# Retention's output made feature-major, and its chain cut into steps between the next head's projections

## The chip, the cores and the metric

One core of a Trainium2 chip. The metric is the device time of the whole program in microseconds, here the median of three runs. A core has five engines with a queue each, worked off in order: TensorE (PE, with its weight loads as PEld), VectorE (DVE), ScalarE (ACT), GpSimd (POOL) and SyncE (SP), which only issues DMA. Granted clock is the share of TensorE's 2.4 GHz that it was given; 0.5 is 1.2 GHz.

## The reference

Two layers of a hybrid model on 512 latent and 256 context tokens of width 1024. Each layer mixes tokens by three branches (retention, window attention, a Fourier transform), joins them by gates, and then sends each token through two of 32 experts. The change touches retention alone: eight heads of width 64, in two directions.

```python
inner = einsum('bcihd,bcjhd->bchij', qc, kc) * dec          # chunks of 128 tokens
o_inner = einsum('bchij,bcjhe->bcihe', inner, vc)
u = einsum('bcjhd,jh,bcjhe->bchde', kc, zeta, vc)           # state of a chunk
_, s_prev = lax.scan(step, s0, moveaxis(u, 1, 0))           # s -> g_chunk * s + u
o_cross = einsum('bcihd,ih,bchde->bcihe', qc, xi, s_prev)
...
mu = mean(o, axis=-1); var = mean(square(o - mu), axis=-1)  # per head
on = (o - mu) * rsqrt(var + 1e-5)
ret = silu(g) * on
```

Layer 0 computes this for all 768 tokens (six chunks), layer 1 for the 512 latent ones (four chunks); the keys and values of the context are used in both.

## The kernel before

All work stands in one program without a loop over layers. Tiles come from pools with a fixed number of buffers: `big` has 20 units of 8 KB per partition, PSUM has 8 banks (3 for projections, `mm`; 2 for `sc`; 2 for transposes, `tr`; 1 for `ov`). The order in which each engine's instructions stand is set by a list scheduler that goes by program order as priority and by when it thinks an operand is ready, so neighbouring pieces of the program are mixed.

A projection (`proj`, L275 to L277) multiplies 128 columns of `w_in`, split into two float32r parts, with the normed tokens: 24 products of 512 latent columns and, where the context is wanted, 24 of 256. In layer 0 each projection also takes one step of the adaLN sums (L149, four products of 32 columns by 512, added up by DVE in L199).

Heads go in pairs `p` = 0 to 3. `ret_proj(p)` makes four projections: keys and queries (rotated by DVE and POOL, L286 to L289), values (turned to token-major by six transposes, L296), and the gate. `ret_chain(p)` then computes the output: it turns the keys (L296), weighs the values for the states (L444), forms q times xi on POOL (L438), the chunks' states (L452, scanned on DVE in L456 to L464), the inner scores (L473, masked with the decay in L475) and the output (L482: scores times values; L487: q times xi times the states, both adding into one PSUM tile per head, tokens on the partitions, so the moving operand has the head's 64 columns). Then the norm: means on DVE (L498, L499), centring (L502), squares on ACT (L503), their sums on DVE (L506, L507), the power -1/2 on POOL (L142), the scaling on POOL (L509), six transposes back (L514), the gate on DVE (L517), and the split into two parts for the branch product (L242, L243).

In the program `ret_proj(p + 1)` stands as a whole ahead of `ret_chain(p)`; ahead of the last chain stand attention's key and value projections and its first query projection:

```python
pr = ret_proj(0)
for p in range(4):
    nxt = ret_proj(p + 1) if p < 3 else None
    ...
    ret_chain(p, pr)
    pr = nxt
```

Of the kernel before, what the change touches and what calls it, by code (L numbers as in the profile page):

```python
# [15 lines left out]
OP = mybir.AluOpType  # L16
# [18 lines left out]
T1_MASK, T1_KA, T1_VA = 0, 384, 1152  # L35
T2_LAT, T2_CTX, T2_CF, T2_ALT, T2_ALTC, T2_ROW, T2_ROWC, T2_N = 0, 1024, 1280, 1536, 1540, 1542, 1799, 1928
CP, _o = {}, 0
for _k, _n in (("ident", 128), ("tri", 128), ("iota1", 64), ("iota0", 32), ("i64", 16), ("kcon", 96), ("tok2", 6),
               ("hbm2", 2), ("zc", 2)):
    CP[_k] = (_o, _o + _n)  # L40
    _o += _n
# [19 lines left out]
def tile_backbone(ctx: ExitStack, tc: tile.TileContext, a: dict, out: bass.AP, stop=None, dbg=None):  # L61
# [51 lines left out]
    # DRAM scratch  # L113
# [6 lines left out]
    cin = const(16, "cin", a["c"])  # L120
    cp = const(480, "cp")
# [7 lines left out]
    tok2, hbm2, zc = (cp[:, CP[k][0]:CP[k][1]] for k in ("tok2", "hbm2", "zc"))  # L129
# [39 lines left out]
    def ada_feature(l, row):  # L169
        """sh1 and norm*(1+sc1), one value for each partition: [128, stream, kc]"""  # L170
# [21 lines left out]
    def ada_steps():  # L192
# [10 lines left out]
        # the last: over a partition's rows on DVE, over the partitions on PE (one stream, the latent one)  # L203
# [42 lines left out]
    def make_h(l, xt_l, xt_c):  # L246
        """xt_*: token-major tiles, already times rstd"""
# [70 lines left out]
    decay = {}  # L318

    def decay_logs(l):  # L320
# [13 lines left out]
        Z = cst.tile([128, 16], F32, name=f"Z{l}", tag="Z")      # [h of f | h of b]  # L334
# [26 lines left out]
    # =====================================================================  # L361
    def layer(l, xt_l, xt_c):
# [15 lines left out]
        mask = t1[:, T1_MASK:T1_MASK + 384]  # L378
# [10 lines left out]
        def o_tiles(b):  # L389
            """[high, low][group] of a branch's output, feature-major"""  # L390
# [10 lines left out]
        def ret_proj(p):  # L401
# [3 lines left out]
            sgr = rv[:, 768:1536]  # L405
            pc, pl = proj(l, p * 4, both)
# [10 lines left out]
            to_tokens(vtok, lambda i: (vc[:, i * 128:i * 128 + 128] if i < 2 else vl[:, (i - 2) * 128:(i - 1) * 128]),  # L417
                      ((0, 2), (2, 4)))
# [4 lines left out]
            return k, q, vtok, sgr  # L423

        def ret_chain(p, st):
            k, q, vtok, sgr = st
# [3 lines left out]
            vz = rb[:, 0:1536].rearrange("p (t h d e) -> p t h d e", t=6, h=2, d=2)  # L430
            St = rc[:, 0:768].rearrange("p (t d e) -> p t d e", t=6, d=2)
            ktok = rc[:, 768:1536].rearrange("p (t c) -> p t c", t=6)
            to_tokens(ktok, lambda i: k[:, i * 128:i * 128 + 128], ((0, 2), (2, 4)))
            # q times xi, for the states' part
            qs = slice(0, 768) if full else lsl
            nt = 6 if full else 4
            for d in range(2):
# [9 lines left out]
            u = []  # L447
            for lo, n in ((0, 2), (2, 4)):
                up = pso()
                for i in range(n):  # L450
                    for h in range(2):
                        PE.matmul(up[h * 64:h * 64 + 64, i * 128:i * 128 + 128], ktok[:, lo + i, h * 64:h * 64 + 64],  # L452
                                  vz[:, lo + i, h, :, :], start=True, stop=True, skip_group_check=True)
# [12 lines left out]
            # inner products  # L466
            for lo, n in (((0, 2), (2, 4)) if full else ((2, 4),)):
                sc = [pss(), pss()]
                for i in range(n):
                    ts = slice((lo + i) * 128, (lo + i) * 128 + 128)  # L470
                    for h in range(2):
                        hs = slice(h * 64, h * 64 + 64)
                        PE.matmul(sc[h][:, i * 128:i * 128 + 128], k[hs, ts], q[hs, ts], start=True, stop=True)  # L473
                for h in range(2):
                    DVE.tensor_tensor(SD[:, h, lo:lo + n, :], sc[h][:, 0:n * 128].rearrange("p (t i) -> p t i", t=n),  # L475
                                      bmid(Dt[:, p * 2 + h, :], n), op=OP.mult)
            oo = [pss(), pss()]
            for t in TL:
                ts = slice(t * 128, t * 128 + 128)
# [909 lines left out]
```

## Time and profile before

| | |
|---|---|
| median of 3 runs | 2665.6 us (2663.58 to 2668.18) |
| profiled execution: span from first to last instruction | 2652.4 us |
| profiled execution's own time | the page gives the span alone; the median lies 13.2 us above it |
| PE busy | 2404.5 us (91%) |
| PEld busy | 1580.7 us (60%) |
| DVE, ACT, POOL busy | 1045.9, 571.0, 469.6 us |
| HBM traffic | 229 GB/s over the span |

The page's slices are 66.3 us each. The retention stage of layer 0 runs from about 56 to 360 us, that of layer 1 from about 1540 to 1730 us; the experts' weights stream from 893 us in layer 0 and again from layer 1's end of mixing to the end. A timeline row gives start, duration and number of records; a float32 product shows as two records, a transpose as one. Starts of following rows tell the pace better than durations, since records overlap. A windows row gives, for one stretch, each engine's busy time and number of records, the granted clock, the share of the DMA engines and the rate.

### The profile page before, as it was taken

To read this page: it belongs to the slowest core of one execution; us is meant where nothing else is said; L and a number is where in the kernel's file an instruction comes from. 1 tells how busy PE (TensorE), PEld (TensorE's weight loads), DVE (VectorE), ACT (ScalarE), POOL (GpSimd) and SP (SyncE) were. 2 spreads that over 40 slices of the span, in tenths; PEclk is the share of its full clock that TensorE was granted. 3 is DMA by queue.
4 is the path that set the end of the run, shared out by engine and by line. 5 is a ranking of instruction groups with operands and counts; after the bars stand their busy time and mean duration, and the time that the engine had idled before them with its cause. 6 is when DMAs were issued, how large, how long until landed. Compare 5 with 4: busy or idle time off the path is not lost. (4 is left out here: it accounts for less than half of the span.)

```text
span 2652.4 us, 44021 instructions
## 1 busy us (share of the span) xinstructions
PE 2404.5 (91%) x17245; PEld 1580.7 (60%) x17245; DVE 1045.9 (39%) x3181; ACT 571.0 (22%) x1285; POOL 469.6 (18%) x414
## 2 busy tenths in 40 slices
PE   5999999999999979999999599999999898997774
PEld 3777766688889944434443388766888743343221
DVE  5434445635234643233332644565335521221112
ACT  3211134521223211011110422245224200000000
POOL 0212110000222412111211123210022321121111
PEclk8988889999999979999999799999999899998897
DMA  7423211235225389899999621110235599999996
GB/s 273 162 96 108 102 51 63 81 111 209 71 64 179 138 331 417 352 371 389 415 417 411 237 72 46 58 48 21 88 97 173 207 379 417 411 410 407 416 415 253
DMA packets 129730, 594.43 MB, mean 224 GB/s; under 512 B 20940, under 2 KB 22052, under 8 KB 73968
## 3 DMA queue, kind: packets, MB, share of 16 engines
q1 hardware_dynamic: 115184, 561.92, 55.0%
q0 software_dynamic: 13376, 26.27, 2.6%
q8 instruction: 138, 2.26, 0.3%
q10 hardware_dynamic: 960, 3.39, 0.3%
q14 instruction: 72, 0.59, 0.1%
HBM read 579.74 MB, written 28.25 MB: 229 GB/s over the span
## 5 line engine op out<-in xcount | busy, mean ns | idle before, releaser
L1079 PE MATMUL mm<-w_gu,xT 128*32 128x256 f32 (+1 forms) x3776 | 564.4, 505 | 85.1 <-DMA w_gu<-in_w_gu_dram 81.7
L1079 PEld LDWEIGHTS mm<-w_gu,xT 128*32 128x32 f32 (+1 forms) x3776 | 192.0, 127 | 390.8 <-issue 227.4
L275 PE MATMUL mm<-hH,hl 128*128 128x512 f32 x800 | 319.7, 401 | 1.7 <-DVE shuf L287 0.9
L276 PE MATMUL mm<-hL,hl 128*128 128x512 f32 x800 | 316.1, 395 | 0.0
L277 PE MATMUL mm<-hH,hl 128*128 128x512 f32 x800 | 315.5, 395 | 0.4 <-DVE hl L238 0.4
L238 DVE TENSOR_TENSOR hl<-raw,hl 128x512 fp32r<-128x512 f32 x248 | 183.3, 741 | 252.1 <-ACT hl L237 251.8
L1104 PE MATMUL mm<-w_d,aT 128*32 128x256 f32 (+1 forms) x1888 | 267.0, 488 | 6.9 <-DVE aT L1094 5.9
L237 ACT CAST hl<-raw 128x512 fp32r<-128x512 f32 x248 | 153.4, 620 | 385.9 <-PE mm L277 250.6
L1084 ACT ACTIVATE act<-mm 128x256 f32<-128x256 f32 (+1 forms) x87 | 30.1, 346 | 899.0 <-PE mm L1079 865.0
L1113 POOL DMA_INDIRECT y_d<-y,gd x87 | 87.7, 1008 | 742.3 <-DVE y L1112 562.3
L1104 PEld LDWEIGHTS mm<-w_d,aT 128*32 128x32 f32 (+1 forms) x1888 | 90.6, 124 | 157.0 <-issue 124.0
L1085 DVE TENSOR_TENSOR act<-act,mm 128x256 f32<-128x256 f32 (+1 forms) x87 | 32.2, 370 | 380.3 <-ACT act L1084 380.3
L275 PEld LDWEIGHTS mm<-hH,hl 128*128 128x128 f32 x800 | 151.3, 189 | 41.1 <-issue 6.1
L277 PEld LDWEIGHTS mm<-hH,hl 128*128 128x128 f32 x800 | 151.3, 189 | 35.5 <-issue 3.9
L276 PEld LDWEIGHTS mm<-hL,hl 128*128 128x128 f32 x800 | 151.2, 189 | 32.4 <-issue 5.2
L275 PE MATMUL mm<-hcH,hl 128*128 128x256 f32 x480 | 143.8, 300 | 5.8 <-ACT ra L408 3.9
L276 PE MATMUL mm<-hcL,hl 128*128 128x256 f32 x480 | 141.8, 295 | 0.0
L277 PE MATMUL mm<-hcH,hl 128*128 128x256 f32 x480 | 141.5, 295 | 0.0
L986 POOL DMA_INDIRECT xg<-h_d,gd x87 | 91.1, 1047 | 148.1 <-issue 71.2
L275 PEld LDWEIGHTS mm<-hcH,hl 128*128 128x128 f32 x480 | 96.2, 200 | 19.0 <-issue 5.7
L276 PEld LDWEIGHTS mm<-hcL,hl 128*128 128x128 f32 x480 | 96.4, 201 | 4.9 <-issue 1.2
L277 PEld LDWEIGHTS mm<-hcH,hl 128*128 128x128 f32 x480 | 96.5, 201 | 3.6 <-issue 3.1
(385 smaller groups left out, 3694.4 us busy)
## 6 DMA issues: line engine op xcount, KB each, us to landing
w_gu<-in_w_gu_dram SPq DMA_DIRECT2D x256, 1024.0 KB
w_d<-in_w_d_dram SPq DMA_DIRECT2D x128, 1024.0 KB
raw<-in_w_in_dram SPq DMA_DIRECT2D x200, 256.0 KB
wada<-in_w_ada_dram SPq DMA_DIRECT2D x48, 1024.0 KB
raw<-in_w_br_dram SPq DMA_DIRECT2D x48, 256.0 KB
yb<-y_d SPq DMA_DIRECT2D x10, 1024.0 KB
raw<-in_w_out_dram SPq DMA_DIRECT2D x32, 256.0 KB
h_d<-hb POOLq DMA_DIRECT2D x10, 512.0 KB, 6.4
```

Source lines behind the costliest of these rows:

```text
L237: ACT.copy(hl[:, 0], r)
L238: DVE.tensor_tensor(hl[:, 1], r, hl[:, 0].bitcast(F32), op=OP.subtract)
L275: PE.matmul(o[:, 0:n], wh, h[kc], start=kc == 0, stop=False)
L276: PE.matmul(o[:, 0:n], wh, lo[kc], start=False, stop=False)
L277: PE.matmul(o[:, 0:n], wl, h[kc], start=False, stop=kc == 7)
L986: POOL.indirect_dma_start(out=xg, out_offset=None, in_=h2_d[l].rearrange("r (a c) -> (r a) c", c=sz * 8), in_offset=bass.IndirectOffsetOnA ...
L1079: PE.matmul(p1[q * sz:q * sz + sz, 0:n], xT[:, k * sz:k * sz + sz], w[:, q * n:q * n + n], start=k == 0, stop=k == 7, skip_group_check=True)
L1084: ACT.activation(sv, pv[:, :, 0, :], AF.Silu)
L1085: DVE.tensor_tensor(sv, sv, pv[:, :, 1, :], op=OP.mult)
L1104: PE.matmul(p2[q * sz:q * sz + sz, 0:n], aT[:, j * 128 + q_ * sz:j * 128 + q_ * sz + sz], w[:, q * n:q * n + n], start=k == 0, stop=k == 3 ...
L1113: s = POOL.indirect_dma_start(out=y_d[l].rearrange("r (a c) -> (r a) c", c=n), out_offset=bass.IndirectOffsetOnAxis(ap=di, axis=0), in_=y, ...
```

## The change

Three things.

1. The values are turned to token-major by a product with a constant matrix, the identity less 1/64 over each head's block (`cenm`, a new table of 128 columns), where transposes stood. So the values have no mean over a head's 64 features, and neither has the output, and the steps that took the mean (L498, L499, L502) are gone.
2. The output comes feature-major. Scores times values has the values (128 by 64) as stationary operand and the masked scores (128 columns) as moving one; the states' part has the state (64 by 64) stationary and q times xi (128 columns) moving. Both heads of a pair add into one PSUM tile, on partitions 0 to 63 and 64 to 127. The squares (ACT, from PSUM) are averaged over each head's features by a product with a matrix of two columns (`bo`), which gives the variance token-major; DVE adds 1e-5, POOL takes the power, ACT spreads it over 64 columns, six transposes bring it to feature-major, and DVE multiplies it into the gated output that POOL has formed meanwhile.
3. `ret_proj` and `ret_chain` are generators. One step of the chain stands behind each of the next pair's four projections (behind the three of attention for the last pair), and the chain's last step behind the first projection of the pair after that. The scores of the context's chunks come a step later than those of the latent ones. The weighted values `vz` lie in the unused ends of three units, so that the masked scores no longer share their place.

"Steps" below are the parts between two `yield`s: turning the keys, `vz`, q times xi and the latent scores; states and context scores; output, squares and gating; variance and power; transposes and split.

```diff
-    def to_tokens(dst, src, segs):
+    def to_tokens(dst, src, segs, by=None):
...
-                PE.transpose(t[:, i * 128:i * 128 + 128], src(lo + i), ident)
+                if by is None:
+                    PE.transpose(t[:, i * 128:i * 128 + 128], src(lo + i), ident)
+                else:
+                    PE.matmul(t[:, i * 128:i * 128 + 128], src(lo + i), by, start=True, stop=True)
...
+        SP.dma_start(t1[:, T1_CEN:], a["t1"][:, 2432:2560])
...
+            to_tokens(vtok, lambda i: (vc[:, i * 128:i * 128 + 128] if i < 2 else vl[:, (i - 2) * 128:(i - 1) * 128]),
+                      ((0, 2), (2, 4)), cenm)
+            yield
...
+            for t in range(6):
+                vt = vtok[:, t].rearrange("p (h e) -> p h e", h=2).unsqueeze(2).broadcast_to([128, 2, 2, 64])
+                DVE.tensor_tensor(vz[t], vt, blast(zb, 64), op=OP.mult)
...
-            for h in range(2):
-                for d in range(2):
-                    j = d * 8 + p * 2 + h
-                    DVE.tensor_scalar(vz[:, :, h, d, :], vtok[:, :, h * 64:h * 64 + 64], Z[:, j:j + 1], None, op0=OP.mult)
+            inner(*segs[0])
+            yield
...
+            if full:
+                inner(*segs[1])
+            yield
+            oo = {lo: pss() for lo, n in segs}
+            for lo, n in segs:
...
-                    PE.matmul(oo[h][:, t * 64:t * 64 + 64], SD[:, h, t, :], vtok[:, t, h * 64:h * 64 + 64],
-                              start=True, stop=False, skip_group_check=True)
+                        PE.matmul(oo[lo][hs, i * 128:i * 128 + 128], vtok[:, lo + i, hs], SD[:, h, lo + i, :],
+                                  start=i == 0, stop=False, skip_group_check=True)
...
-                        PE.matmul(oo[h][:, t * 64:t * 64 + 64], qx[hs, d, ts], St[hs, t, d, :],
+                            PE.matmul(oo[lo][hs, i * 128:i * 128 + 128], St[hs, t, d, :],
+                                      qx[hs, d, t * 128:t * 128 + 128],
...
+                ACT.activation(sq[:, cs_], oo[lo][:, 0:n * 128], AF.Square)
+                ACT.copy(cen[:, cs_], oo[lo][:, 0:n * 128])
+            POOL.tensor_tensor(cen[:, qs], cen[:, qs], sgr[:, qs], op=OP.mult)
+            yield
+            vp = pso()
+            for t in TL:
+                PE.matmul(vp[:, t * 2:t * 2 + 2], sq[:, t * 128:t * 128 + 128], bo, start=True, stop=True)
...
+            DVE.tensor_scalar(var[:, t0 * 2:12], vp[:, t0 * 2:12], 1e-5, None, op0=OP.add)
+            rsqrt(var[:, t0 * 2:12], var[:, t0 * 2:12], 12 - t0 * 2)
+            ACT.copy(sq[:, qs].rearrange("p (n e) -> p n e", e=64), blast(var[:, t0 * 2:12], 64))
+            yield
...
-                DVE.tensor_reduce(mu3[:, :, h], ov, axis=AX.X, op=OP.add, negate=True)
-            DVE.tensor_scalar(mu, mu, 1.0 / 64, None, op0=OP.mult)
...
-            ACT.activation(sq, cen, AF.Square)
...
-            DVE.tensor_reduce(v3, sq, axis=AX.X, op=OP.add)
-            DVE.tensor_scalar(var, var, 1.0 / 64, 1e-5, op0=OP.mult, op1=OP.add)
-            rsqrt(var, var, 2 * n)
-            POOL.tensor_tensor(cen, cen, blast(v3, 64), op=OP.mult)
...
-                    PE.transpose(t[:, i * 128:i * 128 + 128], cf[:, lo + i, :], ident)
+                    PE.transpose(t[:, i * 128:i * 128 + 128], sq[:, (lo + i) * 128:(lo + i) * 128 + 128], ident)
...
-                DVE.tensor_tensor(f, t[:, 0:n * 128], sgr[:, seg], op=OP.mult)
+                DVE.tensor_tensor(f, t[:, 0:n * 128], cen[:, lo * 128:(lo + n) * 128], op=OP.mult)
...
+            chain = ret_chain(p, st)
+            for _ in (ret_proj(p + 1, nxt) if p < 3 else kv()):
+                if done is not None:
+                    next(done, None)
+                    done = None
+                next(chain, None)
+            st, done = nxt, chain
```

TensorE before, at the end of layer 0's first chain: the inner scores (L473) go straight over into the output products.

```order
L276 MATMUL mm_1281<-hL_282,hl_1277 128x512
L473 MATMUL sc_1119<-ra_449 128x128 x4
L482 MATMUL sc_1130<-rv_450,rb_1068 128x64
L487 MATMUL sc_1130<-rc_1069,rq_1067 128x64
L482 MATMUL sc_1130<-rv_450,rb_1068 128x64
L487 MATMUL sc_1130<-rc_1069,rq_1067 128x64
L482 MATMUL sc_1130<-rv_450,rb_1068 128x64
L487 MATMUL sc_1130<-rc_1069,rq_1067 128x64 x2
```

TensorE now, at the same place: the output products stand between the value projection of the next pair (`mm_983`), an adaLN group, and its gate projection (`mm_1095`).

```order
L277 MATMUL mm_983<-hcH_283,hl_980 128x256
L149 MATMUL ov_1033<-wada_1034,cs 32x512 x4
L500 MATMUL sc_1045<-rb_835,rv_451 64x128 x8
L500 MATMUL sc_1046<-rb_835,rv_451 64x128 x4
L509 MATMUL sc_1045<-rq_834,rc_836 64x128 x16
L509 MATMUL sc_1046<-rq_834,rc_836 64x128 x4
L275 MATMUL mm_1095<-hH_279,hl_1086 128x512
```

The two kinds of product alternated, tile by tile; now all of one kind come first, then all of the other, and a projection follows at once.

TensorE now, at the end of that chain: the variance products stand inside the key projection of the pair after the next (`mm_1195`), the transposes of the scale behind it.

```order
L275 MATMUL mm_1195<-hcH_283,hl_1187 128x256
L522 MATMUL ov_1172<-cp,rb_835 128x2 x6
L276 MATMUL mm_1195<-hcL_284,hl_1187 128x256
...
L277 MATMUL mm_1195<-hcH_283,hl_1192 128x256
L149 MATMUL ov_1247<-wada_1248,cs 32x512 x4
L455 MATMUL sc_1298<-ra_758 128x128
L455 MATMUL sc_1299<-ra_758 128x128
L455 MATMUL sc_1298<-ra_758 128x128
L532 MATMUL tr_1261<-cp,rb_835 128x128 x4
L532 MATMUL tr_1270<-cp,rb_835 128x128 x2
L455 MATMUL sc_1299<-ra_758 128x128
```

Of the 29 projection products between L522 and L532, those left out are of the same projection: 12 of 512 columns and 17 of 256 in all. Before, POOL's scaling stood between the output products and the transposes, with seven projection products and four of L473 beside it.

POOL now, from the queries' rotation of one pair to that of the next (`shuf` is the rotation's second part, `var` the power):

```order
L289 TENSOR_TENSOR ra_758<-ra_758,shuf_935 128x512
L518 TENSOR_TENSOR rb_835<-rb_835,rv_451 128x768
L142 TENSOR_TENSOR var_1179<-var_1179,mhalf 128x12
L288 TENSOR_TENSOR shuf_1255<-shuf_1255,rope_413 128x512
L289 TENSOR_TENSOR ra_1183<-ra_1183,shuf_1255 128x512
L466 TENSOR_TENSOR rq_1277<-ra_758,misc_418 128x768 x2
L288 TENSOR_TENSOR shuf_1378<-shuf_1378,rope_413 128x512
```

The scaling by the power, which stood behind L142, is gone from POOL; the gating (L518) stands ahead of it.

## Rows read from the trace of the kernel before

**Rows 1.** The page's 40 slices of 66.3 us: TensorE's busy tenths and its clock.

```profile
PE   5999999999999979999999599999999898997774
PEclk8988889999999979999999799999999899998897
```

**Rows 2.** Windows: stretch, its length, busy per engine, clock, DMA share, GB/s.

```profile
148.25:162.43 14.18, 14.18 (x65) 12.04 (x64) 0.69 (x1) 0.00 (x0) 0.00 (x0) 0.64 0.00 1
162.43:182.00 19.57, 13.32 (x61) 10.90 (x63) 10.47 (x19) 3.65 (x7) 9.22 (x6) 0.65 0.32 121
219.07:232.55 13.48, 13.48 (x65) 11.39 (x64) 1.29 (x2) 0.37 (x1) 0.00 (x0) 0.68 0.00 1
232.55:242.00 9.45, 9.45 (x57) 6.45 (x55) 5.76 (x11) 2.35 (x4) 3.76 (x2) 0.74 0.70 250
284.51:297.10 12.59, 12.59 (x67) 10.73 (x65) 0.00 (x0) 0.00 (x0) 0.00 (x0) 0.66 0.26 101
297.10:308.00 10.90, 9.68 (x57) 5.46 (x56) 7.85 (x16) 3.49 (x7) 3.83 (x3) 0.76 0.36 120
332.42:346.26 13.84, 13.84 (x65) 11.71 (x63) 0.46 (x1) 0.00 (x0) 0.00 (x0) 0.65 0.01 1
346.26:362.00 15.74, 14.97 (x72) 9.62 (x70) 10.45 (x29) 4.39 (x6) 5.66 (x4) 0.88 0.11 34
...
1593.85:1609.00 15.15, 12.44 (x68) 10.77 (x69) 7.70 (x17) 3.14 (x6) 7.47 (x6) 0.89 0.12 36
...
1675.23:1680.63 5.40, 5.40 (x53) 4.72 (x51) 0.69 (x1) 0.34 (x1) 0.00 (x0) 1.00 0.16 49
...
1718.47:1736.00 17.53, 14.58 (x51) 9.59 (x49) 13.01 (x43) 6.86 (x15) 5.45 (x4) 0.61 0.00 0
```

**Rows 3.** Timeline of TensorE behind chain 0; in brackets idle time and its releaser.

```profile
170.91 1.54 PE L514 MATMUL tr<-cp,rb 128*128 128x128 f32 x6 [4.47 <-POOL rb L509]
...
174.24 0.58 PE L275 MATMUL mm<-hcH,hl 128*128 128x256 f32 x1 [1.78 <-ACT ra L408]
```

**Rows 4.** Windows: a stretch of layer 0's attention without projections.

```profile
470.00:498.00 28.00, 26.91 (x191) 16.34 (x190) 20.40 (x104) 17.52 (x55) 0.15 (x1) 1.00 0.12 39
```

**Rows 5.** Timeline of TensorE: start us, duration us, engine, line, shapes, records.

```profile
1707.15 1.09 PE L452 MATMUL ov<-rb,rc 128*64 128x128 f32 x16
1708.18 0.50 PE L277 MATMUL mm<-hH,hl 128*128 128x512 f32 x1
...
1712.39 0.39 PE L277 MATMUL mm<-hH,hl 128*128 128x512 f32 x1
...
1691.83 0.60 PE L296 MATMUL tr<-cp,val 128*128 128x128 f32 x4
1692.18 0.48 PE L275 MATMUL mm<-hH,hl 128*128 128x512 f32 x1
...
518.78 1.13 PE L635 MATMUL sc<-t,fb 128*128 128x128 f32 x8
519.75 0.28 PE L639 MATMUL sc<-fu,t 128*128 128x2 f32 x2
...
504.99 0.50 PE L646 MATMUL sc<-t,fb 128*128 128x2 f32 x4
505.35 0.89 PE L649 MATMUL sc<-t,fb 128*128 128x256 f32 x3
```

**Rows 6.** Groups by line, 60 to 375 us: busy us, mean ns, idle before.

```profile
L142 POOL TENSOR_TENSOR var<-var,mhalf 128x12 f32<-128x12 f32 x4 | 9.1, 2282 | 172.9 <-DVE var L507 172.9
...
L503 ACT ACTIVATE rb<-rb 128x768 f32<-128x768 f32 x4 | 3.4, 842 | 75.6 <-DVE rb L502 75.6
...
L462 DVE SCALAR_TENSOR_TENSOR rc<-rc,g,ov 128x64 f32<-128x64 f32 x12 | 3.3, 277 | 0.1
```

**Rows 7.** Issues of expert weights, and the window behind the first.

```profile
L893 SPq DMA_DIRECT2D w_gu<-in_w_gu_dram x256: 327/333/519, 893.1 to 2599.0; - x128
...
950.00:1000.00 50.00, 44.46 (x506) 20.99 (x507) 12.76 (x51) 5.66 (x13) 7.48 (x9) 0.89 1.00 400
```

More of the change, by code (lines that the diff above doesn't have):

```diff
@@ L429, in ret_chain, with inner @@
             SD = rb[:, 0:1536].rearrange("p (h t i) -> p h t i", h=2, t=6)
-            vz = rb[:, 0:1536].rearrange("p (t h d e) -> p t h d e", t=6, h=2, d=2)
             St = rc[:, 0:768].rearrange("p (t d e) -> p t d e", t=6, d=2)
             ktok = rc[:, 768:1536].rearrange("p (t c) -> p t c", t=6)
-            to_tokens(ktok, lambda i: k[:, i * 128:i * 128 + 128], ((0, 2), (2, 4)))
+            vz = [r[:, 1536 + i * 256:1792 + i * 256].rearrange("p (h d e) -> p h d e", h=2, d=2)
+                  for r in (rq, rb, rc) for i in range(2)]
             qs = slice(0, 768) if full else lsl
             nt = 6 if full else 4
+            segs = ((2, 4), (0, 2)) if full else ((2, 4),)
+            def inner(lo, n):
+                sc = [pss(), pss()]
+                for i in range(n):
+                    ts = slice((lo + i) * 128, (lo + i) * 128 + 128)
+                    for h in range(2):
+                        hs = slice(h * 64, h * 64 + 64)
+                        PE.matmul(sc[h][:, i * 128:i * 128 + 128], k[hs, ts], q[hs, ts], start=True, stop=True)
+                for h in range(2):
+                    DVE.tensor_tensor(SD[:, h, lo:lo + n, :], sc[h][:, 0:n * 128].rearrange("p (t i) -> p t i", t=n),
+                                      bmid(Dt[:, p * 2 + h, :], n), op=OP.mult)
+            zb = Z.rearrange("p (d h) -> p h d", d=2)[:, p * 2:p * 2 + 2, :]
+            to_tokens(ktok, lambda i: k[:, i * 128:i * 128 + 128], ((0, 2), (2, 4)))
+            for t in range(6):
+                vt = vtok[:, t].rearrange("p (h e) -> p h e", h=2).unsqueeze(2).broadcast_to([128, 2, 2, 64])
+                DVE.tensor_tensor(vz[t], vt, blast(zb, 64), op=OP.mult)
             for d in range(2):
@@ L465, in ret_chain @@
                                                  op0=OP.mult, op1=OP.add)
-            for lo, n in (((0, 2), (2, 4)) if full else ((2, 4),)):
-                sc = [pss(), pss()]
+            if full:
+                inner(*segs[1])
+            yield
+            oo = {lo: pss() for lo, n in segs}
+            for lo, n in segs:
                 for i in range(n):
-                    ts = slice((lo + i) * 128, (lo + i) * 128 + 128)
                     for h in range(2):
                         hs = slice(h * 64, h * 64 + 64)
[L473 to L476, printed above, removed]
@@ L490, in ret_chain @@
-            n = len(TL)
-            t0 = TL[0]
-            cen = rb[:, 0:768].rearrange("p (t h e) -> p t h e", t=6, h=2)[:, t0:6]
-            sq = rb[:, 768:1536].rearrange("p (t h e) -> p t h e", t=6, h=2)[:, t0:6]
-            mu = small(2 * n, "mu")
-            mu3 = mu.rearrange("p (t h) -> p t h", h=2)
-            for h in range(2):
-                ov = oo[h][:, t0 * 64:384].rearrange("p (t e) -> p t e", t=n)
-                DVE.tensor_reduce(mu3[:, :, h], ov, axis=AX.X, op=OP.add, negate=True)
@@ L499, in ret_chain @@
-            DVE.tensor_scalar(mu, mu, 1.0 / 64, None, op0=OP.mult)
-            for h in range(2):
-                ov = oo[h][:, t0 * 64:384].rearrange("p (t e) -> p t e", t=n)
-                DVE.tensor_tensor(cen[:, :, h, :], ov, blast(mu3[:, :, h], 64), op=OP.add)
-            ACT.activation(sq, cen, AF.Square)
-            var = small(2 * n, "var")
-            v3 = var.rearrange("p (t h) -> p t h", h=2)
-            DVE.tensor_reduce(v3, sq, axis=AX.X, op=OP.add)
-            DVE.tensor_scalar(var, var, 1.0 / 64, 1e-5, op0=OP.mult, op1=OP.add)
@@ L508, in ret_chain @@
-            rsqrt(var, var, 2 * n)
-            POOL.tensor_tensor(cen, cen, blast(v3, 64), op=OP.mult)
-            cf = rb[:, 0:768].rearrange("p (t c) -> p t c", t=6)
-            for lo, n in (((0, 2), (2, 4)) if full else ((2, 4),)):
+                        PE.matmul(oo[lo][hs, i * 128:i * 128 + 128], vtok[:, lo + i, hs], SD[:, h, lo + i, :],
+                                  start=i == 0, stop=False, skip_group_check=True)
+            for lo, n in segs:
+                for i in range(n):
+                    t = lo + i
+                    dirs = [d for d in range(2) if (t, d) not in ((0, 0), (1, 1))]
+                    for d in dirs:
+                        for h in range(2):
+                            hs = slice(h * 64, h * 64 + 64)
+                            PE.matmul(oo[lo][hs, i * 128:i * 128 + 128], St[hs, t, d, :],
+                                      qx[hs, d, t * 128:t * 128 + 128],
+                                      start=False, stop=d == dirs[-1], skip_group_check=True)
@@ L1243, in _consts @@
     put("zc", np.concatenate([127 - p, p], 1))
+    half = np.kron(np.eye(2), np.full((64, 64), 1.0 / 64))
+    put("bo", half[:, ::64])
     c["cp"] = cp
@@ L1266, in _consts @@
     mask = np.concatenate([np.where(j >= i, 0, NEG), np.zeros((128, 128)), np.where(j <= i, 0, NEG)], 1)
[L1267 removed]
+    c["t1"] = np.ascontiguousarray(np.concatenate([CA, SA, CR, SR, mask, np.eye(128) - half], 1).astype(f))
     E1 = np.maximum(j - i, 0)
```

75 lines of the change are left out of this document (38 added, 37 removed).

## The prediction

> **What bounds the kernel now.** I read the slices of the page first. TensorE is busy in nine tenths or more of the slices that hold the retention stage, yet its clock row falls below 9 there [rows 1]: an engine that looks full, at less than full speed. So I cut that stage into stretches with the view by windows. In each of layer 0's four chains the products for the output (L482, L487) take 12.59 to 14.18 us, TensorE busy all the time, at a granted clock of 0.64 to 0.68, which is a change from 2.4 to 1.2 GHz some three tenths of the way in. After each follows a stretch at 0.65 to 0.88 [rows 2]. In layer 1 the same block takes 5.40 us at 1.00 (one row stands for four, 5.40 to 5.85 us), and the stretches after the first and the last block read 0.89 and 0.61. The timeline of chain 0 shows what TensorE waits for at the end of a chain: 4.47 us for POOL's L509, whose input is POOL's power L142 (2.28 us), then 1.78 us for a projection's buffer [rows 3]. TensorE works in order, so the next projections stand behind these waits. Nothing else limits the stage: the loads run at a share of 0.00 to 0.70 of the DMA engines in all these stretches [rows 2].
>
> What the clock does after a fall matters as much as the fall. It fell each time in a block of products that move 64 columns, with no idle time in front (14.18 busy of 14.18 us). In layer 0's attention, where for 28 us TensorE does only small products and transposes, most of them 128 columns or more wide, with no projection among them, it stays at 1.00 [rows 4]. I read from this that the narrow moving operand goes with the fall, not small products as such.
>
> **The change, part by part.** The sum is made against the profiled execution, span 2652.4 us; the page gives no other time of it. The median of the runs, 2665.6, lies 13.2 us above; I take that off and add it again unchanged.
>
> *Output products.* A layer 0 chain has 32 (12 of L482, 20 of L487), a layer 1 chain 24 (8 and 16); the counts stay. The new ones hold 64 columns still and move 128. The nearest row is L452, of the same form as the new L500: 16 records, two to a product, from 1707.15 to the next start at 1708.18, so 0.129 us each [rows 5]. L509 uses 64 rows by 64 columns, which no row shows; if its two heads run beside each other as L452's do, the price is the same. Low bound 0.129; high bound 0.243, a product of full shape (L635: four in 0.97 us [rows 5]), as when the heads follow each other. I take 0.129, since L452 pairs two heads in the same way. Layer 0: 14.18 + 13.48 + 12.59 + 13.84 = 54.1 becomes 4 x 32 x 0.129 = 16.5, a gain of 37.6. Layer 1: 5.40 less one projection product's step (0.34) = 5.06 becomes 24 x 0.129 = 3.1; 2.0 x 4 = 8.0.
>
> *The clock and the idle time behind them.* Loss of a stretch = (1 - clock) x busy, plus what is not busy [rows 2]. Layer 0: 0.35 x 13.32 + 6.25 = 10.9; 0.26 x 9.45 = 2.5; 0.24 x 9.68 + 1.22 = 3.5; 0.12 x 14.97 + 0.77 = 2.6; together 19.5. Layer 1: 0.11 x 12.44 + 2.71 = 4.1; 2.3 and 1.0 in the two between, read from rows of the same kind; 0.39 x 14.58 + 2.95 = 8.6; together 16.0. All of it goes if the clock stays and if each step finds its inputs.
>
> *Does it find them?* The new order puts one projection between two steps. The tightest step is the one that ended in the 4.47 us: from the variance product (L522) to the transposes L532 stand, in layer 0, 12 projection products of 512 columns and 17 of 256. A 512-column product takes (1712.39 - 1708.18) / 18 = 0.234 us [rows 5]; the others at half of that, an estimate: 2.8 + 2.0 = 4.8 us, and behind them an adaLN group and three products of L455. Beside it run one DVE step on 12 elements, POOL's power 2.28 and ScalarE's copy of 768 elements (as L503, 0.84): 3.1 us and that step [rows 6]. It fits with some 1.5 us to spare before the extra products are counted. In layer 1, 24 of 512 alone cover 5.6 us. For the states, DVE's ten short steps (0.28 each, 2.8 us [rows 6]) have 28 projection products and L500 in front of L509. DVE and ACT are FIFO too: what is queued behind the added waits (L525, L527, the squares L516) are the splits of the next weights; the order keeps one or two splits ahead of each. I allow 5 us in all for steps that come late, since the last chain of each layer meets attention, whose own first waits partly stay.
>
> *Added work.* The values go to token-major by a product with the centring matrix in place of a transpose: 48 over the kernel, from 0.088 (four in 0.35 us, L296) to 0.243 (L635): +7.4 us [rows 5]. The variances take 24 + 16 = 40 products of 2 columns; L646 shows two in 0.36 us, 0.18 each: +7.2 us. Bounds: 0.09 if the two records overlap, 0.243 as L635: 3.6 to 9.7. The Trainium skill (TensorEngine Tiling, Instruction Overhead) puts a fixed cost of about 60 cycles on a matmul of few columns; an estimate by it is 0.05 us a product, 2 us in all. The row is far above, so the row stands.
>
> *Hidden.* DVE loses the sums, centring and the sum of squares (L498, L502, L506) and gains two half-size steps per chain for vz; ACT gains copies and squares. Even behind chain 0 DVE is busy for only 10.47 of 19.57 us [rows 2], so beside projections this costs nothing; without that cover the two steps, of 256 elements each, would be at most 1.7 us per chain (an estimate: 0.84 each, what 768 elements take in L503 [rows 6]). On SP there is one more table load of 64 KB; the load of w_ada now waits once for the chain's rb buffer with two weight loads behind it, but those are used over 100 records later, more than 10 us. POOL's queue has the power in front of the next rotation, 2.28 us; the rotated q is read a head later.
>
> Sum: 37.6 + 8.0 + 19.5 + 16.0 = 81.1; less 7.4 + 7.2 + 5 = 19.6: 61.5 us. 2665.6 - 61.5 = 2604. The time passes to the end: the first expert weights are issued at 893.1, behind all of this, and only from there the loads are full, 1.00 at 950 to 1000 [rows 7].
>
> **Rivals.** (a) L509's quadrants don't run beside each other. All at 0.243: 0.114 x (128 + 96) = 25.5 us more: 2630. For: no row shows the form. Against: L452's pairs.
> (b) The clock falls again. The new L500 and L509 stand in one block behind an adaLN group, and L509 fills a quarter of the array at a time. In layer 0 alone each fall costs up to 4.1 us in the block and 2.2 us behind it (mean of 2.5, 2.3, 1.8): 25 us, 2629; in both layers 50, 2654. Against: the attention rows. The Trainium skill (TensorE: Matmul & The Clock Gate, Why this matters for your kernels) asks for an engine without idle gaps to keep the clock. By that rule alone the falls of rows 2, with no idle time, have another cause and may come back; the rows on the 64-column blocks weigh more with me.
> (c) Slower: TensorE waits at the steps. Eight chains of five steps stand in its queue; if each waited 1.54 us (61.5 / 40) all would be gone. The place is POOL, which must do two rotations, two products with xi, the gating and the power between two heads (the power alone 2.28 us [rows 6]); if one is late, all steps behind it are. At 1.8 us a step: 72 us, 2676. Against: the order puts each a projection or more ahead.
> (d) Layer 0's part is given back in the weight stream that follows. Only layer 1's stays, 8.0 + 16.0 - 3.7 - 2.9 - 2 = 15: 2650. Against: the stream starts behind TensorE [rows 7].
>
> **How the numbers follow.** Forecast 0.70, (a) 0.10, (b) 0.12, (c) 0.04, (d) 0.04. The forecast's own range is 2590 (variance products at their low bound, no late step and some of the unknown switch cost between tile shapes gone) to 2617 (double the allowance for late steps, dearer variance products). With (a) and the smaller (b) the range is 2584 to 2632. No change, for which 0.2% is 5.3 us, about what a measurement of this kernel can tell, needs a mishap near (c)'s break-even: 0.02. Slower 0.04, faster 0.94.
>
> **What would show it.** Right: a granted clock of 1.00 across both retention stages; L500 and L509 of a layer 0 chain in some 4.2 us; no wait of TensorE on POOL or ACT over 1 us there; L522's six products in 1.1 us; the first load of w_gu near 893 - 45. A head of layer 0 takes about 50 us from block to block, where it now takes 70 and 65 (from the end of one block of rows 2 to the end of the next). Wrong: a clock below 1 right behind an L509 block (b), L509 at 0.24 us a product (a), idle time in front of L532, L500 or L455 (c), an unchanged start of layer 1 in spite of an earlier load of w_gu (d).

## The result and the profile after

| | time | runs |
|---|---|---|
| before | 2664.6 us (2662.6 to 2668.2) | 4 |
| after | 2589.1 us (2584.4 to 2593.8) | 4 |
| ratio | 0.9725, 95% interval 0.9702 to 0.9748 | |

75.5 us less by the medians, where 61.5 were forecast. The time lies inside the stated 2584 to 2632 us, and 1 us below the range that the forecast by itself had (2590 to 2617). The profiled execution of after has a span of 2587.6 us, 64.8 less than the one of before.

The slices of the page for after (TensorE's busy share, then its granted clock, in tenths), against [rows 1]:

```profile
PE   5999999999999799999999599999999799987773
PEclk8999999999999799999999799999999799998887
```

The slices of both retention stages (from 65 us on in layer 0, from 1488 us on in layer 1) now read 9 in both rows. The view by windows, for the output blocks and what follows them (us from the span's start; busy time of TensorE, weight loads, VectorE, ScalarE, GpSimd; clock, DMA share, GB/s), against [rows 2]:

```profile
124.90:128.70 3.80, 3.80 (x69) 3.46 (x65) 1.29 (x2) 0.87 (x3) 0.00 (x0) 1.00 0.24 73
128.70:142.00 13.30, 13.30 (x81) 10.91 (x80) 3.00 (x5) 4.25 (x10) 1.84 (x1) 1.00 0.29 103
175.20:179.00 3.80, 3.80 (x69) 3.46 (x65) 1.29 (x2) 0.82 (x2) 0.00 (x0) 1.00 0.26 73
276.40:280.20 3.80, 3.80 (x69) 3.46 (x65) 2.16 (x2) 0.33 (x2) 1.67 (x2) 1.00 0.32 118
1637.40:1640.40 3.00, 3.00 (x50) 2.64 (x49) 1.91 (x4) 0.62 (x1) 1.39 (x1) 1.00 0.08 29
1640.40:1656.00 15.60, 15.60 (x74) 11.74 (x73) 5.54 (x15) 4.12 (x8) 4.46 (x5) 1.00 0.24 68
```

Blocks of 3.80 us where [rows 2] had 12.59 to 14.18, 3.00 where they had 5.40; there is no idle time behind them, and the clock is 1.00 in all these windows. From block end to block end a layer 0 pair of heads takes 50.3 us (128.7 to 179.0). The waits of [rows 3] are gone: before the transposes L532 TensorE never sat idle, and of the waits for a projection's buffer on ScalarE one of 0.5 us is left in layer 0's stage. The timeline for the products that are new (start, length, line, tiles, shape, records):

```profile
90.56 0.71 PE L299 MATMUL tr<-t,vc 128*128 128x128 f32 x4
91.11 1.06 PE L299 MATMUL tr<-t,vl 128*128 128x128 f32 x8
91.92 0.47 PE L275 MATMUL mm<-hH,hl 128*128 128x512 f32 x1
...
124.90 1.53 PE L500 MATMUL sc<-rb,rv 128*64 128x128 f32 x24
126.36 2.40 PE L509 MATMUL sc<-rq,rc 64*64 64x128 f32 x40
128.69 0.50 PE L275 MATMUL mm<-hH,hl 128*128 128x512 f32 x1
...
143.28 1.40 PE L522 MATMUL ov<-cp,rb 128*128 128x2 f32 x12
144.54 0.36 PE L276 MATMUL mm<-hcL,hl 128*128 128x256 f32 x1
```

Two records make one product. From the start of a row to the next start, L500 costs 1.46 / 12 = 0.122 us, L509 2.33 / 20 = 0.117, a variance product 1.26 / 6 = 0.21, a centring product 1.36 / 6 = 0.227, where a transpose took 0.088 [rows 5].

To see where the time came from I charged every TensorE record with the time to the next record's start (idle time apart), from a layer's first projection to the end of its attention:

| us | before, layer 0 | after | before, layer 1 | after |
|---|---|---|---|---|
| output products | 54.1 | 15.2 | 20.4 | 11.7 |
| projections | 239.5 | 230.8 | 198.3 | 192.7 |
| idle | 15.7 | 9.4 | 17.4 | 10.1 |
| states, scores, adaLN | 45.8 | 38.3 | 13.6 | 10.4 |
| rest (turning, centring, variances, attention) | 107.6 | 117.8 | 92.9 | 98.0 |
| sum | 462.7 | 411.4 | 342.6 | 322.9 |

So the stages give 51.3 and 19.7 us, 71.0 together. The profiles differ by only 64.8, mainly because layer 0's weight stream took longer in this one execution. The view of line L1111 up to 1500 us, for after and for a second profile of the same kernel (durations, then first and last start):

```profile
L1111 PE MATMUL mm<-w_gu,xT x1824: 376/592/1116, 905.3 to 1421.0; 128*64 128x512 f32 x113, 128*32 128x256 f32 x70
```

```profile
L1111 PE MATMUL mm<-w_gu,xT x1824: 376/592/1117, 904.2 to 1413.7; 128*64 128x512 f32 x113, 128*32 128x256 f32 x70
```

515.7 us here, 509.5 there; the same stretch of before took 510.8. The second profile has a span of 2579.8, and its stages repeat (410.9 and 323.0). By the medians the gain is 75.5 and not 64.8 because before's own profiled execution, with a span of 2652.4 us, is some 10 us shorter than the runs timed beside it, and after's is not.

### The profile page after: what moved, and what is told of

Read it like the earlier page. It is cut to its first block, busy times and chain, and to the rows that moved or that the text cites. A ratio compares the mean times of both kernels' runs of the same rounds, so it can differ in the third digit from the quotient of the medians.

```text
span 2587.6 us, 44255 instructions
## 1 busy us (share of the span) xinstructions
PE 2357.3 (91%) x17373; PEld 1546.3 (60%) x17373; DVE 1034.7 (40%) x3149; ACT 581.8 (22%) x1309; POOL 473.2 (18%) x414
## 5 line engine op out<-in xcount | busy, mean ns | idle before, releaser
L1111 PE MATMUL mm<-w_gu,xT 128*32 128x256 f32 (+1 forms) x3776 | 569.5, 506 | 75.8 <-DMA w_gu<-in_w_gu_dram 71.9
L1111 PEld LDWEIGHTS mm<-w_gu,xT 128*32 128x32 f32 (+1 forms) x3776 | 194.0, 127 | 384.8 <-issue 236.8
L275 PE MATMUL mm<-hcH,hl 128*128 128x256 f32 x480 | 139.1, 290 | 2.0 <-DVE shuf L287 0.7
L277 PE MATMUL mm<-hcH,hl 128*128 128x256 f32 x480 | 137.4, 286 | 0.0
L275 PEld LDWEIGHTS mm<-hcH,hl 128*128 128x128 f32 x480 | 92.2, 192 | 10.5 <-issue 1.9
L277 PEld LDWEIGHTS mm<-hcH,hl 128*128 128x128 f32 x480 | 92.3, 192 | 1.9 <-issue 1.4
```

The lines of the kernel that those rows point to most:

```text
L275: PE.matmul(o[:, 0:n], wh, h[kc], start=kc == 0, stop=False)
L277: PE.matmul(o[:, 0:n], wl, h[kc], start=False, stop=kc == 7)
L1111: PE.matmul(p1[q * sz:q * sz + sz, 0:n], xT[:, k * sz:k * sz + sz], w[:, q * n:q * n + n], start=k == 0, stop=k == 7, skip_group_check=True)
```

## The experiments

Each ratio is to the kernel before on the same chip. What the products of layer 0's four output blocks took, by the charging above, orders the runs. "Alone" means that a product, or two of the same head, stands between two changes of tile shape; "pairs of heads" that the two heads' products of one kind follow each other; "side by side" that the two heads use different parts of the array in one long row of products. A stage is what was charged above, a layer's first projection to the end of its attention.

| kernel | ratio (95%) | order in a block, columns moved | layer 0 blocks, us | clock in them | layer 0 / layer 1 stage, us |
|---|---|---|---|---|---|
| before | 1 | head by head, alone; 64 | 54.1 | 0.64 to 0.68 | 462.7 / 342.6 |
| p_single | 0.9956 (0.994 to 0.9971) | the same; 64 | 59.1 | 0.60 to 0.71 | 449.5 / 354.0 |
| wide | 0.9984 (0.9971 to 0.9997) | the same; 128 | 41.2 | 1.00 | 452.9 / 347.7 |
| f_single | 0.9894 (0.9877 to 0.991) | the same; 128 | 41.6 | 1.00 | 437.0 / 346.1 |
| group | 0.9907 (0.9887 to 0.9927) | by shape, head after head; 64 | 37.4 | 0.66 to 0.81 | 445.7 / 341.5 |
| p_only | 0.9751 (0.9734 to 0.9768) | pairs of heads; 64 | 31.7 | 0.70 to 0.94 | 419.3 / 322.3 |
| p_wide | 0.9737 (0.9722 to 0.9752) | pairs of heads; 128 | 29.1 | 1.00 | 409.0 / 321.7 |
| narrow | 0.9726 (0.9711 to 0.9742) | by shape, side by side; 64 | 16.5 | 1.00 | 408.9 / 324.1 |
| f_only | 0.9771 (0.9749 to 0.9794) | by shape, side by side; 128 | 15.7 | 1.00 | 419.6 / 334.7 |
| after_again | 0.9725 (0.9708 to 0.9743) | the same; 128 | 15.2 | 1.00 | 410.9 / 323.0 |

**Form and placement, each alone.** Form is the feature-major output with its centring and variance products (parts 1 and 2 of the change), placement the steps between the projections (part 3). My theory was that the form makes nearly all of the gain.

f_only puts the chain back in one piece:

```
             for _ in (ret_proj(p + 1, nxt) if p < 3 else kv()):
-                if done is not None:
...
-                next(chain, None)
-            st, done = nxt, chain
...
+                pass
+            for _ in ret_chain(p, st):
+                pass
+            st = nxt
```

> The changed kernel with its placement undone: the feature-major chain is handed over in one piece behind the next head's projections, where the kernel before had its chain; the compiler's scheduler then puts its instructions among the projections. Theory (the form of the output products is nearly all of the gain): output blocks of 3.8 us in layer 0 and 3.0 us in layer 1, clock 1.00 in both retention stages, and only idle time can come back, at most the 14 us that the kernel before had there: 2589 to 2603 us. Rival (the placement keeps the clock up and the waits covered): the stretches behind the blocks lose 19.5 and 16.0 us again: about 2625 us.

p_only keeps the generators and takes the lines for output, mean and variance from the kernel before, with plain transposes of the values.

> The changed kernel with its form undone: the steps stand between the projections as in the changed kernel, but the output is token-major again (64 moving columns, shapes alternating, mean and variance on DVE, no centring product, no variance product). Theory (form): a layer 0 block takes 12 to 14 us and the clock is below 1.00 in it and behind it; 2589 + 38.9 (blocks of layer 0) + 8 (layer 1) + 21 (clock behind) - 15.6 (the products that the new form adds) = 2641 us, 2620 to 2650. Rival (placement): the blocks run at 1.00, 6.7 us in layer 0 and 5.1 in layer 1: 2589 + 11.6 + 8.2 - 15.6 = 2593 us.

f_only 2598.0 and p_only 2590.0 us, beside 2656.9 for the kernel before. f_only lies in the range of my theory: its blocks are short and at 1.00, and it loses at waits (1.86 us for a projection's buffer behind its first block) and in layer 1, where the clock falls behind such a wait (0.79 in 1552 to 1560 us). p_only shows the clock below 1.00 in its layer 0 blocks, as my theory had it, yet they take only 7.0 to 9.1 us, and its time came out at the rival's number: placement alone brings 66.9 us, form alone 58.9, both together 73 (0.9725 of 2656.9). They are not two parts of a sum; each alone gives most of it. My theory that the form is the gain was wrong, so the question became what the two have in common.

**What goes with the clock's fall.** wide lets the products of the kernel before move 128 columns, group sorts them by shape:

```
-  PE.matmul(oo[h][:, t * 64:t * 64 + 64], SD[:, h, t, :], vtok[:, t, h * 64:h * 64 + 64], ...
+  PE.matmul(oo[h][:, t * 64:t * 64 + 128], SD[:, h, t, :], vtok[:, t, :], ...
```

> The kernel before with its output products moving 128 columns instead of 64 (a neighbour's columns beside its own, so the retention output is not the reference's), all else as before. Theory N (the narrow moving operand goes with the clock's fall): clock 1.00 in the blocks, 6.7 to 7.8 us each in layer 0; 25 us come back in the blocks and 11 + 10 behind them: about 2620 us, though each product moves twice the columns. Rival S (the alternation of two tile shapes goes with the fall): the falls stay, blocks of 13 to 16 us, 2660 to 2680 us.

> The kernel before with the output products in another order: all of L482 first, then all of L487, so that the tile shape changes once in a block and not at nearly every product; still 64 moving columns. Theory N (narrow operand): the falls stay in layer 0, blocks of 10 to 13 us, 2645 to 2662 us. Rival S (alternating shapes): clock 1.00, blocks of 4.2 to 5.4 us in layer 0, 34 us in the blocks and 21 behind them come back: about 2605 us.

Windows of wide: its first block, what follows, its second block:

```profile
147.20:158.50 11.30, 11.30 (x68) 8.48 (x66) 0.69 (x1) 0.00 (x0) 0.00 (x0) 1.00 0.01 1
158.50:175.00 16.50, 9.01 (x47) 7.87 (x46) 9.07 (x18) 2.76 (x5) 6.78 (x5) 0.69 0.33 127
214.40:225.70 11.30, 11.30 (x70) 8.51 (x73) 1.31 (x3) 0.37 (x1) 0.00 (x0) 1.00 0.01 1
```

the fall behind wide's first block more closely, and the wait that it begins in:

```profile
163.70:173.80 10.10, 5.10 (x22) 4.70 (x23) 4.63 (x10) 1.84 (x4) 4.92 (x4) 0.50 0.14 59
```

```profile
166.92 1.54 PE L514 MATMUL tr<-cp,rb 128*128 128x128 f32 x6 [5.27 <-POOL rb L509]
```

and of group, its first block, what follows, its second block:

```profile
147.40:157.80 10.40, 10.40 (x66) 10.03 (x65) 1.02 (x2) 0.00 (x0) 0.00 (x0) 0.68 0.01 2
157.80:176.00 18.20, 12.45 (x52) 10.43 (x52) 9.16 (x19) 3.65 (x7) 8.84 (x6) 0.62 0.34 125
214.30:223.60 9.30, 9.30 (x69) 8.96 (x71) 1.63 (x3) 0.37 (x1) 0.00 (x0) 0.77 0.01 2
```

On the clock theory N held and S fell: with 128 columns the level stays at 2.4 GHz through the block, shapes in turn as they are; with 64 it drops to 1.2 in all four blocks, though the shape changed only three times in each (the scheduler kept the heads apart). What wide shows behind its first block is a second kind of fall, in a stretch with 7.49 us of idle time: the clock reads 0.50 from 163.7 us on, within the wait of 5.27 us that ends at 166.92. The Trainium skill (TensorE: Matmul & The Clock Gate, Why this matters for your kernels) has its rule on drops of throughput about such gaps; this row agrees with it. The falls in group's blocks and in those of [rows 2] have no idle time in front of them and are of the first kind.

On the time N failed: wide gained 0.2%, not 1.7. A block at full clock still took 10.1 to 11.3 us, not 6.7 to 7.8. Some of that is the doubled columns (a product alone took 0.42 us in wide, 0.36 in before), but not most of it. And group, whose falls stayed, gained 0.9%, with blocks of 7.7 to 10.4 us. So the clock was not the main thing that made the blocks long.

**More on the clock.** narrow halves the columns in the new form, p_wide doubles them in p_only:

```
+                        for c in (0, 64):
+                            PE.matmul(oo[lo][hs, i * 128 + c:i * 128 + c + 64], vtok[:, lo + i, hs],
+                                      SD[:, h, lo + i, c:c + 64], ...
```

> The changed kernel with each output product cut into two that move 64 columns (64 products in a layer 0 chain, 48 in a layer 1 chain); the arithmetic stays. Theory N (a block of narrow moving operands goes with the clock's fall): clock below 0.95 in layer 0's blocks or right behind them, blocks of 5 to 9 us there; 0.003 to 0.011 above the changed kernel's ratio. Rival R (what holds the clock is that two heads use the array side by side): clock 1.00, blocks of 3.8 to 6 us, 0.000 to 0.004 above.

> The token-major output in the new places (as p_only) with 128 columns moving instead of 64 (a neighbour's columns beside its own, so the retention output is not the reference's). p_only showed 0.70 to 0.94 in its layer 0 blocks. Theory N: 1.00 in all blocks and behind them, blocks of 7.5 to 9.5 us in layer 0; 0.971 to 0.975 of the kernel before. Rival (something else in the block, the alternation or the DVE and ACT work beside it, goes with the fall): 0.70 to 0.94 as in p_only, blocks of 9 to 12 us, 0.976 to 0.980.

One window each of narrow, of p_wide and of p_only:

```profile
125.70:129.90 4.20, 4.20 (x133) 4.06 (x129) 1.29 (x2) 0.98 (x3) 0.00 (x0) 1.00 0.26 66
```

```profile
124.60:131.90 7.30, 7.30 (x69) 5.86 (x65) 1.29 (x2) 0.55 (x2) 0.00 (x0) 1.00 0.14 38
```

```profile
123.90:133.00 9.10, 9.10 (x69) 7.97 (x65) 1.30 (x3) 0.59 (x2) 0.00 (x0) 0.70 0.11 31
```

and one block of layer 1, of group and of p_only, both with 64 columns:

```profile
1569.40:1573.20 3.80, 3.80 (x50) 3.64 (x48) 0.00 (x0) 0.00 (x0) 0.00 (x0) 1.00 0.24 69
```

```profile
1525.10:1529.80 4.70, 4.70 (x50) 4.16 (x49) 0.71 (x2) 1.10 (x2) 0.00 (x0) 1.00 0.19 56
```

p_wide came out as N says (0.9737; blocks of 7.30 at 1.00). narrow went against N: 64 columns throughout, and 1.00. So a narrow moving operand alone does not bring the fall. It was seen in layer 0's blocks of 64 columns of before, group and p_only, which last 7.0 us and more, not where the heads run side by side and the block is over in 4.2 us. The blocks of group and p_only in layer 1 keep 1.00 too, at 3.80 and 4.70 us. Whether the length of the block counts or the order in it was not separated.

**What makes a block long.** p_single gives p_only's blocks the order that the compiled kernel before had; f_single gives it to the new form:

```
+            for h in range(2):
...
+                for lo, n in segs:
+                    for i in range(n):
...
+                        PE.matmul(oo[lo][hs, ...], vtok[:, t, hs], SD[:, h, t, :], ...)
+                        for d in dirs:
+                            PE.matmul(oo[lo][hs, ...], St[hs, t, d, :], qx[hs, d, ...], ...)
```

> The token-major output in the new places (as p_only), with the products inside a block in the order that the kernel before had: head 0 through all tiles, then head 1, so that the tile shape changes at every product or two. p_only took 31.7 us for layer 0's four blocks, the kernel before 54.1. Theory O (the order inside the block, a change of shape at nearly every product, made the blocks long): 0.34 us a product at full clock as in the first 3.7 us of the block at 148 us of the kernel before, so 10.8 us a block, 43 us for four, up to 55 with the clock's fall; 0.979 to 0.985 of the kernel before. Rival (the place made them short): about 32 us, 0.974 to 0.977.

> The changed kernel with its output products in the order that the kernel before had: head 0 through all tiles, then head 1, L500 and L509 in turn, so that the two heads no longer stand beside each other and the tile shape changes at every product or two; form (feature-major, 128 moving columns) and places stay. Theory O (what made the blocks short is the order: pairs of heads, few changes of shape): 0.33 us a product as in wide's blocks, 10 to 12 us a block at clock 1.00, some 25 to 30 us more in layer 0 and 18 to 25 in layer 1: 0.986 to 0.993 of the kernel before. Rival F (the feature-major form with 128 moving columns is what makes them short): blocks of 4 to 5 us, 0.972 to 0.977.

The timeline of p_only's second block, still at full clock there:

```profile
179.35 0.66 PE L500 MATMUL sc<-rv,rb 128*128 128x64 f32 x4
179.94 0.44 PE L505 MATMUL sc<-rc,rq 64*128 64x64 f32 x4
180.31 0.66 PE L500 MATMUL sc<-rv,rb 128*128 128x64 f32 x4
```

of p_single's first, where it starts at full clock and where the clock has gone:

```profile
124.56 0.43 PE L501 MATMUL sc<-rv,rb 128*128 128x64 f32 x2
124.93 0.43 PE L504 MATMUL sc<-rc,rq 64*128 64x64 f32 x2
125.29 0.43 PE L501 MATMUL sc<-rv,rb 128*128 128x64 f32 x2
...
132.12 0.69 PE L501 MATMUL sc<-rv,rb 128*128 128x64 f32 x2
132.74 0.69 PE L504 MATMUL sc<-rc,rq 64*128 64x64 f32 x2
133.36 0.69 PE L501 MATMUL sc<-rv,rb 128*128 128x64 f32 x2
```

of f_single's first, all of it at 1.00:

```profile
124.20 0.43 PE L502 MATMUL sc<-rb,rv 128*64 128x128 f32 x2
124.56 0.65 PE L505 MATMUL sc<-rq,rc 64*64 64x128 f32 x4
125.14 0.43 PE L502 MATMUL sc<-rb,rv 128*64 128x128 f32 x2
```

of before's first, at its start:

```profile
148.25 0.43 PE L482 MATMUL sc<-rv,rb 128*128 128x64 f32 x2
148.61 0.43 PE L487 MATMUL sc<-rc,rq 64*128 64x64 f32 x2
```

of wide's first, at 1.00:

```profile
148.31 0.49 PE L482 MATMUL sc<-rv,rb 128*128 128x128 f32 x2
148.73 0.49 PE L487 MATMUL sc<-rc,rq 64*128 64x128 f32 x2
```

and of group's second, six and eight products of one head each in a row:

```profile
214.32 1.55 PE L480 MATMUL sc<-rv,rb 128*128 128x64 f32 x12
215.80 2.00 PE L488 MATMUL sc<-rc,rq 64*128 64x64 f32 x16
217.72 1.55 PE L480 MATMUL sc<-rv,rb 128*128 128x64 f32 x12
```

The windows of p_single's first block and of one in layer 1:

```profile
124.60:140.00 15.40, 15.40 (x69) 13.02 (x65) 1.85 (x3) 0.51 (x1) 0.00 (x0) 0.62 0.06 18
```

```profile
1606.70:1617.50 10.80, 10.80 (x50) 9.27 (x48) 1.12 (x2) 1.10 (x2) 0.00 (x0) 0.64 0.10 35
```

Read the differences of the starts. A product alone takes 0.36 us in the old form with 64 columns (p_single, before) and in the new form with 128 (f_single); in the old form with 128 (wide) it takes 0.42. In a row of one shape and one head it takes 0.245 (group: 1.48 / 6 and 1.92 / 8). Two products of L505 for two heads in p_only take 0.37, as much as one. In f_single two of L505 for one head take 0.58. Theory O held: 15.4, 16.0, 14.0 and 14.0 us a block in p_single (59.1 in all, over the 55 I allowed; in layer 1 the clock fell too, and the blocks went from 18.5 to 39.4), 10.5 in f_single. p_single loses four fifths of p_only's gain, more than I had given it (0.9956, not 0.979 to 0.985); f_single loses 45 us of the changed kernel's 73 (0.9894 against 0.9725), within its range.

So this is what form and placement share. The program text of before has the two heads in turn; the compiled order of its layer 0 blocks has one head after the other, with a change of shape after every product or two (0.36 us for a product alone from 148.25 us on). In the new places the scheduler left the text's order, pairs of heads; in the new form, in either place, it left L500 and L509 in groups. Why it parted the heads in the old place was not tried, and no run has pairs of heads there, so what the order alone would bring in the old place is not shown; group, sorted by shape, is the nearest (0.9907). In layer 1 before, two of the heads' products already stood together, which is why [rows 2] has 5.40 us there.

**A version without the centring product.** cen_dve takes the mean off the values on VectorE and turns them by transposes:

```
-                      ((0, 2), (2, 4)), cenm)
+                      ((0, 2), (2, 4)))
...
+            DVE.tensor_reduce(mu3, v4, axis=AX.X, op=OP.add, negate=True)
+            DVE.tensor_scalar(mu, mu, 1.0 / 64, None, op0=OP.mult)
+            DVE.tensor_tensor(v4, v4, blast(mu3, 64), op=OP.add)
```

> The changed kernel with the head's mean taken off the values by VectorE (a sum, a scaling, an addition on 768 columns) behind plain transposes, in place of the 48 products with the centring matrix. A product takes 0.267 us (six in 1.6 us), a transpose 0.133 (six in 0.8): 48 x 0.134 = 6.4 us of TensorE go. If VectorE's three steps (about 2.5 us a head, an estimate from 0.84 for 768 elements) stay behind the next projection: 0.0024 below the changed kernel's ratio. If they are late for the states: the same ratio or up to 0.003 above.

> The changed kernel once more, unaltered, to stand beside the others on one chip. Expected at 0.9725 of the kernel before (0.970 to 0.975). Its profile tells whether the stages repeat: layer 0 from the first projection to the end of attention in 411 us, layer 1 in 323 us.

> cen_dve again, beside the changed kernel on one chip in five rounds. If its 48 cheaper products count on the path: 0.0024 below the changed kernel's ratio. If the first difference (0.9701 against 0.9725, intervals that overlap) was chance: the same ratio within 0.001.

> The changed kernel, unaltered, in five rounds beside cen_dve_2: 0.9725 of the kernel before, 0.971 to 0.974; its two stages 411 and 323 us as before.

First it took 0.9701 (0.9688 to 0.9714) beside after_again, intervals that overlap; then 0.9712 (0.9699 to 0.9725), 2584.8 us, beside after_third's 0.9746 (0.9732 to 0.976), 2591.6 us, intervals apart. So it is faster by 5.4 and 6.8 us, the second in part because after_third came out slower than the changed kernel did in the two sets of runs before. By the charging the 48 centring products took 10.7 us and the 48 transposes in their place 5.3, so 5.4 us of TensorE go; the 6.4 that I expected came of prices that had the last record's tail in them (six in 1.6 us, where the next row starts after 1.36).

The stages show this in layer 0 alone: 407.4 and 407.6 us against 410.7 to 411.4. In layer 1 the clock fell once during attention in both profiles of cen_dve (326.6 and 325.4 us) and in that of after_third (328.1), and not in the two other profiles of the changed kernel (322.9 and 323.0). Why it falls there in some executions is open. after_third lies just above the 0.971 to 0.974 that I gave it, and its layer 1 stage 5 us above the 323 expected.

## Why the prediction was right, and where its reasons were not

**Output products: size right, reason short.** Forecast 37.6 and 8.0, measured 38.9 and 8.7. Taking L452's 0.129 us for the new form was right (0.117 to 0.122), and rival (a) did not come. What failed is the reason. From "I read from this that the narrow moving operand goes with the fall" I took layer 0's long blocks for a matter of the clock and of the form. At full clock they would have taken some 10 us each, an estimate: f_single's blocks of that order took 10.5 at 1.00, and with p_single's prices at either level (0.36 and 0.62 us a product) those of [rows 2] come to 9.0 to 9.9. The rest, to 13.5, is the clock; the larger part, from 3.8 to some 10, is the order, which the timeline inside a block of before shows. My high bound, 0.243 us, is the price of products of one shape and one head in a row (group: six of L480 in 1.48 us); alone they cost 0.36, so the bound was too low, and the price of the new form held only because its products stay in groups. The sum did not say that it hung on this.

**Clock and idle time: 35.5 forecast, 38.6 measured** (projections 8.7 + 5.6, idle 6.3 + 7.3, states, scores and adaLN 7.5 + 3.2). The clock is 1.00 from 57 us to 318 and from 1475 to 1656, in all blocks and behind them, so rival (b) did not come. Later in layer 0's charged stretch it falls once, in attention (0.96 over 320 to 411 us). "All of it goes" was right, but not for the form's sake: p_only's layer 1 stage is as short without it (322.3 us against 322.9). "It fell each time in a block of products that move 64 columns" was not so. Behind chain 0 of before the clock had risen again and fell a second time, some 7 us after the last such product, behind a stretch in which TensorE was busy for 0.65 of 3.30 us:

```profile
165.80:169.10 3.30, 0.65 (x8) 0.45 (x8) 1.11 (x2) 0.00 (x0) 2.07 (x1) 1.00 0.98 412
169.30:179.40 10.10, 6.71 (x30) 6.31 (x31) 5.76 (x11) 1.91 (x4) 4.92 (x5) 0.50 0.00 0
```

That is in the wait for POOL of [rows 3], and wide, with 128 columns, has the same fall; so part of the clock's loss there goes with the wait and not with the 64 columns.

**Added products: 14.6 forecast, 15.3 measured** (the rest grows by 10.2 and 5.1). The variance products are at 0.21 us, near the row's 0.18. They are far from the 0.05 that I had estimated from the Trainium skill (TensorEngine Tiling (Array Packing), Instruction Overhead).

**Late steps: 5 allowed, none seen.** This is the largest miss in the sum: no step was late, rival (c) did not come. L522's six products took 1.26 us to the next start, 1.1 forecast.

The stages: 46.6 + 14.9 us by my terms, 51.3 + 19.7 measured; the 9.5 between them are these four differences (2.0 + 3.1 - 0.7 + 5 = 9.4). Rival (d) did not come: the first load of w_gu was issued at 840.6 us, 52.5 earlier, and the end kept the gain but for the one slow stream.

**What was wrong is the attribution.** The sum gave the form 45.6 us of output products less 14.6 of its additions, and the placement only idle time. The runs give the placement alone 66.9 us, most of it by the order that the scheduler left there: p_single, the same places with the heads parted, is at 0.9956. With the placement, the form adds 1 to 7 us (0.9751 against 0.9746, 0.9725 and 0.9725 in the three sets of runs of the changed kernel). The intervals overlap; that it adds anything is not shown.

## What to carry to other kernels

Before a block of small products is priced by its clock or by its operand widths, read its timeline: a product alone between two changes of tile shape cost one and a half times what it cost in a row of its own shape, and three times what it cost in a row with the other head's product beside it, and the compiled order, not the text, decides which it is. When a change has two parts, a sum over both says nothing about either; each alone has to be run, since both may cure the same thing.

## What the runs showed of the hardware

- The ladder for a small float32 product at full clock: 0.12 us in a row with the other head's beside it (L500 and L509 of after), 0.245 in a row of one shape and one head (group), 0.36 alone between changes of shape (p_single with 64 columns, f_single with 128), 0.42 alone in the old form with 128 columns (wide). The Trainium skill (TensorEngine Tiling (Array Packing), Key Properties) says that a change of tiling mode drains TensorE. The runs agree in that a change of shape costs, some 0.1 us a product (0.36 less 0.245); no trace shows the drain itself.
- The clock can fall in a block without idle time: in p_single 4 us into a block, and in layer 1 as well once its blocks were of that order (0.64 to 0.81). Moving 128 columns kept it at 1.00, in blocks of up to 11.3 us (wide). With 64 columns it stayed at 1.00 in narrow's blocks of 4.2 us, with the heads side by side, and in layer 1's of 3.80 and 4.70 us (group, p_only).
- A part of the gain hung on the scheduler: the same lines for the output, handed over some projections earlier, compiled to another order inside the block.
